# The first raw loads of the mixer's weights wait for a left operand of group 4

## The chip, the cores and the metric

The kernel runs on one NeuronCore of a Trainium2 chip. Its engines work side by side: TensorE (PE in the profile; its weight loads are PEld) multiplies matrices, VectorE (DVE), ScalarE (ACT) and GpSimd (POOL) work elementwise, and SyncE (SP) issues most DMA transfers. DMA issues also stand in ScalarE's queue (ACTq). An engine runs its instructions in order, and a DMA whose data or buffer isn't ready holds up what is queued behind it on the same issuing queue. The metric is the device time of one execution in microseconds. Before the change its median is 1780.38 us over 3 runs (1780.27 to 1782.05).

## The reference

One decoder layer on x of 1024 tokens by 1024 features, in float32:

```python
x = layernorm(ALPHA * x + 0.5 * swiglu(x, ffn1_w1, ffn1_w3, ffn1_w2))
m = mixer(x, w_in, ..., w_uk, w_uv, ..., ws, bs, w_out)
x = layernorm(ALPHA * x + m)
x = layernorm(ALPHA * x + 0.5 * swiglu(x, ffn2_w1, ffn2_w3, ffn2_w2))

def swiglu(x, w1, w3, w2):          # hidden width 2816
    return (silu(x @ w1) * (x @ w3)) @ w2
```

The mixer projects x with `w_in`, runs sparse attention (an indexer picks 256 of the causal keys per query, the attention works on latent keys and values of width 128) on one half and a chunked gated MLP on the other, and projects the result with `w_out`.

## The kernel before

**Splits.** A float32 product is made of three matmuls on split operands: `split` writes hi = the operand rounded to the matmul's format (ScalarE, L87) and lo = operand - hi (VectorE or GpSimd, L88), and `mm3` (L149 to L153) adds hi x hi, hi x lo and lo x hi in one PSUM tile.

**Stage 1 of the first feed-forward part** computes silu(x w1) * (x w3) in 11 groups (NG) of hidden columns. In each group a 2x2 block product is done with 7 block products instead of 8; the left operands are sums of the w13 weights (four loads of 512 KB per group, L341, issued one group ahead; sums in `left`, L287 to L292; then their split), the right operands are sums of x, made once (`xs`). A block product is 24 matmuls. For groups 0 to 5 the products m = 1 and 2 are computed ahead of all else ("early"; the results are spilled and read back, L433 and L434), so these groups have 5 products left, in the order 6, 7, 5, 4, 3 (group 0: 6, 5, 7, 3, 4); groups 6 to 10 have 7, in the order 1, 6, 2, 7, 5, 4, 3. There are two pairs of PSUM banks (`ab`), so a product waits until VectorE has added up the product two before it: L381 takes product 6, L412 and L415 use products 7 and 5, L422 product 4, L428 product 3 (group 0 has L392 to L405 for some of these). `gated` (L348, L349) applies silu and the product, `out` (L439 to L449) forms the seven sums of the hidden block and stores them to DRAM (`f`).

**The mixer's weights** are split ahead of time, beside stage 1. `make_parts` is a generator over 29 weights. For each it issues the load of the next raw weight on SP (L116, up to 512 KB), splits the present one on ScalarE and VectorE (tile `made`) and stores the pair to DRAM from ScalarE's queue (L136, up to 1 MB). `product` calls it four times per block product (L329, L330), one step each; six steps make one weight. A list scheduler then sets the order on each engine by dependences and estimated times, so that a load which depends on nothing can move ahead of where it was written.

**Buffers.** Raw weights and the `hid` loads of stage 2 share one ring of two buffers (`raw`, N_W = 2), in program order. The split pairs, the `xs` pairs and the W2 weights share a pool of 15 large buffers.

**Stage 2** multiplies by W2: 11 loads of 1 MB (L503, `w_446` to `w_456`), loads of the stored hidden sums (`hid`, L551, two pieces of 256 KB in one), their splits into a and b, and W2 sums on VectorE (L524, L525). Its pieces (m, k) are worked in a fixed order, (1,0), (1,1), (1,2) and so on, with 12 matmuls each (tile y for these).

Of the kernel before, what the change touches and what calls it, by code (L numbers as in the profile page):

```python
# [7 lines left out]
F32 = mybir.dt.float32  # L8
# [5 lines left out]
ALU = mybir.AluOpType  # L14
# [17 lines left out]
N_W = PAR["NW"]  # L32
N_BIG = PAR["NB"]
EARLY = 6
class Net:
# [63 lines left out]
    def make_parts(self):  # L99

        nc, ins = self.nc, self.ins
        flat = lambda x: x.rearrange("p k c -> p (k c)")
        todo = [(("T", i), flat(ins["w_inT"][i])) for i in (6, 4, 5)]
        todo += [((n, j), flat(ins["w_in" + n][j])) for n in "ABC" for j in range(4)]
        todo += [("ws", flat(ins["wsT"]))]
        todo += [(("T", i), flat(ins["w_inT"][i])) for i in range(2)]
        todo += [(("O", i), ins["w_out"][i]) for i in range(4, 8)]
        todo += [(("T", i), flat(ins["w_inT"][i])) for i in range(2, 4)]
        todo += [("wuk", flat(ins["w_ukT"]))]
        todo += [(("O", i), ins["w_out"][i]) for i in range(4)]  # L110
        raws = {}

        def load(i):
            if i < len(todo):
                raws[i] = self.raw("made", (P, todo[i][1].shape[-1]))
                nc.sync.dma_start(raws[i], todo[i][1])  # L116

        load(0)
        for i, (key, src) in enumerate(todo):
            x, n = raws[i], src.shape[-1]  # L120
            load(i + 1)
            if key == "ws":
                y = x.rearrange("p (g c) -> p g c", g=NH)
                nc.gpsimd.affine_select(
                    out=y, in_=y, pattern=[[0, NH], [1, P]], compare_op=ALU.is_ge, fill=0.0, base=0, channel_multiplier=-1
                )
            if key == "wuk":
                nc.scalar.activation(x, x, AF.Copy, scale=0.125)
            yield
            t = self.large("made", (P, 2, n))  # L130
            self.split(x, t[:, 0], t[:, 1])
            yield
            yield
            name = self.name("made")
            self.made[key] = self.dram.tile([P, 2, n], F32, tag=name, name=name)
            nc.scalar.dma_start(self.made[key], t.bitcast(F32))  # L136
            for _ in range(3):
                yield
# [117 lines left out]
    def ffn(self, name, w13, w2, begin, meanwhile, load_acc, norm, after, side=iter(())):  # L256
# [21 lines left out]
        def left(n):  # L278

            for g, m in plan[len(lefts) : n]:  # L280
                if g < EARLY and m in (1, 2):
                    lefts[g, m] = self.parts(first_blocks[g, m], V)
                    continue
                a = blocks[g]
                if m == 6:
                    a[5] = self.page("S", (P, 2, HALF))
                    V.tensor_tensor(a[5], a[7], a[4], ALU.add)  # L287
                    a[6] = a[1]
                    V.tensor_tensor(a[7], a[1], a[7], ALU.subtract)
                    V.tensor_tensor(a[6], a[5], a[1], ALU.subtract)  # L290
                if m == (5 if g else 3):
                    V.tensor_tensor(a[2], a[2], a[6], ALU.subtract)  # L292
                    a[3] = a[2]
                lefts[g, m] = self.parts(a[m], E(PAR["LE"][m - 1] if g > 1 else 0))

        def halves(j):

# [16 lines left out]
        def product(g, m, ps, start=True):  # L314
            now = plan.index((g, m))
            for k in range(4):
# [9 lines left out]
                for j in range(2):  # L326
                    ks = slice(k * P, (k + 1) * P)
                    self.mm3(ps[:, j], (w[0][:, j, ks], w[1][:, j, ks]), x, start and k == 0, k == 3, m in (1, 2, 3, 5))
                if g > 1 and now > 2 * EARLY:  # L329
                    next(side, None)  # L330

        def load(g, m, s=slice(0, 2), of=None):
# [901 lines left out]
```

## Time and profile before

| | |
|---|---|
| median of 3 runs | 1780.38 us |
| the profiled execution's own time | 1782.18 us |
| its span on the core | 1780.5 us |
| TensorE busy | 1728.8 us (97%) |
| VectorE busy | 1330.2 us (75%) |
| ScalarE busy | 792.0 us (44%) |
| GpSimd busy | 394.1 us (22%) |
| mean DMA rate | 163 GB/s |

The profile shows one execution. Its span runs from the first to the last instruction on the core, and the time of that execution is 1.7 us longer. Busy times of the engines overlap. A wait names the instruction that released it. Line numbers are those of the kernel before; in the changed kernel the lines from L116 on are 3 higher and those after the left operands 4 higher (the raw load is L119, the L88 split is unmoved, L381 is L385, L503 is L507, L551 is L555).

### The profile page before, as it was taken

The numbers are of one execution on the slowest core, as the hardware profiler recorded it, in microseconds if no ns is written. First come the engines' busy times: TensorE is split into PE (matmuls) and PEld (weight loads), VectorE is DVE, ScalarE is ACT, GpSimd is POOL, SyncE is SP. The second block draws the span as 40 slices with busy tenths as digits, with TensorE's granted clock in tenths as the row PEclk, the third lists the DMA queues.
The fourth block names the chain that finished last, engine by engine and source line by source line (L and its number), as shares of the span: only waits on it lengthen the run. The fifth ranks groups of instructions, "written<-read, shape, count | busy, mean of one in ns | idle before, by whom it ended". The sixth has DMA issues, their size and how long they took to land.

```text
span 1780.5 us, 22284 instructions
## 1 busy us (share of the span) xinstructions
PE 1728.8 (97%) x8056; PEld 1449.9 (81%) x8056; DVE 1330.2 (75%) x2213; ACT 792.0 (44%) x1328; POOL 394.1 (22%) x287
## 2 busy tenths in 40 slices
PE   8989999999999999999978999999999999999997
PEld 6878888888888889998866888888788888888886
DVE  5778886765895864699889877877877555589586
ACT  5433333333654524568687662452313222354551
POOL 0004332222000460011246421100423222200036
PEclk9999999999999999999999999999999999999999
DMA  7458777758545342225412006435443322753532
GB/s 285 154 213 318 256 262 276 280 204 305 192 122 173 107 184 95 96 84 198 169 36 95 1 1 212 154 119 188 157 178 121 136 89 89 288 195 118 181 101 83
DMA packets 90141, 289.96 MB, mean 163 GB/s; under 512 B 9136, under 2 KB 9648, under 8 KB 85680
## 3 DMA queue, kind: packets, MB, share of 16 engines
q1 hardware_dynamic: 82496, 253.12, 40.1%
q10 hardware_dynamic: 5616, 32.54, 4.6%
q0 software_dynamic: 1920, 2.89, 0.8%
q8 instruction: 63, 1.03, 0.2%
q14 instruction: 46, 0.38, 0.1%
HBM read 195.94 MB, written 89.69 MB: 160 GB/s over the span
## 4 chain that ended last, share of the span: by engine, by line
PE 71%; DVE 7%; ACT 4%; DMA 2%; issue 2%; POOL 1%; SPq 0%; POOLq 0%; ACTq 0%; DVEq 0%
PE ab L151 11%; PE ab L153 11%; PE ab L152 11%; PE y L152 5%; PE y L153 5%; PE y L151 5%; PE z L153 3%; PE z L152 3%; PE z L151 3%; ACT act L828 2%; PE pN L153 2%; PE pN L151 2%; PE pN L152 2%; PE tr L1006 1%; PE lg L702 1%
## 5 line engine op out<-in xcount | busy, mean ns | idle before, releaser
L151 PE MATMUL ab<-xs,hi 128*128 128x512 f32 x1232 | 482.4, 392 | 18.4 <-DVE c L415 6.7
L152 PE MATMUL ab<-xs,hi 128*128 128x512 f32 x1232 | 481.2, 391 | 0.0
L153 PE MATMUL ab<-xs,lo 128*128 128x512 f32 x1232 | 481.0, 391 | 0.0
L151 PEld LDWEIGHTS ab<-xs,hi 128*128 128x128 f32 x1232 | 232.6, 189 | 69.7 <-issue 12.5
L152 PEld LDWEIGHTS ab<-xs,hi 128*128 128x128 f32 x1232 | 232.6, 189 | 48.9 <-DVE xs L88 0.4
L153 PEld LDWEIGHTS ab<-xs,lo 128*128 128x128 f32 x1232 | 232.5, 189 | 48.6
L88 POOL TENSOR_TENSOR lo<-w,hi 128x1024 fp32r<-128x1024 f32 x54 | 137.9, 2553 | 568.6 <-ACT hi L87 531.2
L87 ACT ACTIVATE hi<-w 128x1024 fp32r<-128x1024 f32 (+1 forms) x134 | 137.6, 1040 | 160.4 <-DVE w L290 126.6
L88 DVE TENSOR_TENSOR lo<-w,hi 128x1024 fp32r<-128x1024 f32 (+1 forms) x80 | 94.7, 1195 | 42.4 <-ACT hi L87 41.9
L88 DVE TENSOR_TENSOR a<-hid,a 128x512 fp32r<-128x512 f32 x132 | 93.3, 707 | 24.2 <-ACT a L87 24.0
L87 ACT ACTIVATE a<-hid 128x512 fp32r<-128x512 f32 x132 | 82.0, 621 | 53.9 <-DMA hid<-f 50.2
L153 PE MATMUL z<-b,a 128*128 128x512 f32 x264 | 102.7, 389 | 0.0
L152 PE MATMUL y<-b,a 128*128 128x512 f32 x264 | 102.7, 389 | 0.0
L153 PE MATMUL y<-b,a 128*128 128x512 f32 x264 | 102.7, 389 | 0.0
L152 PE MATMUL z<-b,a 128*128 128x512 f32 x264 | 102.7, 389 | 0.0
L151 PE MATMUL z<-b,a 128*128 128x512 f32 x264 | 102.5, 389 | 0.0
L88 DVE TENSOR_TENSOR b<-w,b 128x512 fp32r<-128x512 f32 x110 | 77.1, 701 | 34.0 <-ACT b L87 33.8
L828 ACT ACTIVATE act<-score,tk 128x768 int8<-128x768 f32 (+2 forms) x93 | 87.0, 935 | 34.2 <-DVE tk L840 27.7
L151 PE MATMUL y<-b,a 128*128 128x512 f32 x264 | 102.0, 389 | 0.0
L87 ACT ACTIVATE b<-w 128x512 fp32r<-128x512 f32 x110 | 68.4, 622 | 51.9 <-PE z L153 38.5
L348 ACT ACTIVATE h<-c 128x512 f32<-128x512 f32 x34 | 21.4, 631 | 152.8 <-DVE c L415 103.3
L592 POOL TENSOR_TENSOR xacc<-xacc,T 128x512 f32<-128x512 f32 x8 | 13.0, 1652 | 333.8 <-DVE T L565 333.8
(264 smaller groups left out, 3586.7 us busy)
## 6 DMA issues: line engine op xcount, KB each, us to landing
w<-in_ffn_w_dram SPq DMA_DIRECT2D x110, 512.0 KB, 6.3
hid<-f SPq DMA_DIRECT2D x60, 512.0 KB, 3.8
w<-in_ffn_w_dram SPq DMA_DIRECT2D x22, 1024.0 KB, 10.3
made<-made ACTq DMA_DIRECT2D x17, 1024.0 KB, 6.3
f<-h SPq DMA_DIRECT2D x32, 512.0 KB, 3.6
f<-c SPq DMA_DIRECT2D x22, 512.0 KB, 3.1
wo<-made SPq DMA_DIRECT2D x8, 1024.0 KB, 6.9
xr<-x_spill SPq DMA_DIRECT2D x16, 512.0 KB, 5.6
```

What stands on the lines that cost most here:

```text
L87: nc.scalar.activation(hi, src, AF.Copy)
L88: (eng or nc.vector).tensor_tensor(lo, src, hi.bitcast(F32), ALU.subtract)
L151: mm(out, a[0], b[0], start=start, stop=False, skip_group_check=skip)
L152: mm(out, a[0], b[1], start=False, stop=False, skip_group_check=skip)
L153: mm(out, a[1], b[0], start=False, stop=stop, skip_group_check=skip)
L348: nc.scalar.activation(t, c[:, 0], AF.Silu)
L592: nc.gpsimd.tensor_tensor(acc[j][:, HALF:], acc[j][:, HALF:], T[j], ALU.add)
L702: self.nc.tensor.matmul(out, l, r, start=n == 0, stop=n == 1)
L828: nc.scalar.activation(out, s, AF.Sign, bias=fj, scale=-1.0, accum_out=val[:, j : j + 1])
L1006: nc.tensor.transpose(pt[:, hh * P : (hh + 1) * P], ps4[hh][:, j * P : (j + 1) * P], self.ident)
```

## The change

`left` remembers the hi tile of the last left operand that it made (`self.recent`). For the first two raw loads, GpSimd first writes two columns of the raw buffer (hi - hi of that operand), so that the DMA, which overwrites them, has to wait for it. And `product` begins to call the generator in group 4 instead of group 2. When the first call comes, the last operand made is that of group 4, product 4.

```diff
@@ make_parts
             if i < len(todo):
                 raws[i] = self.raw("made", (P, todo[i][1].shape[-1]))
+                if i < N_W:
+                    t = self.recent.bitcast(F32)[:, 0, :2]
+                    nc.gpsimd.tensor_tensor(raws[i][:, :2], t, t, ALU.subtract)
                 nc.sync.dma_start(raws[i], todo[i][1])
@@ left
                 lefts[g, m] = self.parts(a[m], E(PAR["LE"][m - 1] if g > 1 else 0))
+                self.recent = lefts[g, m][0]
@@ product
-                if g > 1 and now > 2 * EARLY:
+                if g > 3 and now > 2 * EARLY:
                     next(side, None)
```

The order of SP's queue around the four w13 loads of group 2 before (`w_110` to `w_113`; `made` are raw loads of the mixer's weights):

```order
L444 DMA f_75<-u_88_651 128x512
L341 DMA w_110_834<-in_ffn_w_dram 128x1024
L341 DMA w_111_836<-in_ffn_w_dram 128x1024
L341 DMA w_112_838<-in_ffn_w_dram 128x1024
L448 DMA f_75<-c_89_652 128x1024
L448 DMA f_75<-h_90_653 128x1024
L341 DMA w_113_840<-in_ffn_w_dram 128x1024
L116 DMA made_1121<-in_w_inA_dram 128x768
L116 DMA made_1172<-in_w_inA_dram 128x768
L449 DMA f_75<-u_88_651 128x512
```

The same place in the changed kernel:

```order
L345 DMA w_110_834<-in_ffn_w_dram 128x1024
L345 DMA w_111_836<-in_ffn_w_dram 128x1024
L345 DMA w_112_838<-in_ffn_w_dram 128x1024
L452 DMA f_75<-c_89_652 128x1024
L452 DMA f_75<-h_90_653 128x1024
L345 DMA w_113_840<-in_ffn_w_dram 128x1024
L453 DMA f_75<-u_88_651 128x512
L448 DMA f_75<-h_104_784 128x512
```

The raw loads behind and between the groups' loads are gone here; the loads of w13 stand behind the same store (`f<-c`).

SP's queue before, at the first hid loads and the first W2 load (`w_446`), in groups 8 and 9:

```order
L116 DMA made_2613<-in_w_out_dram 128x1024
L551 DMA hid_3126<-f_75 128x2x512
L446 DMA f_75<-h_359_2396 128x1024
L551 DMA hid_3140<-f_75 128x2x512
L448 DMA f_75<-c_374_2477 128x1024
L448 DMA f_75<-h_375_2478 128x1024
L449 DMA f_75<-u_373_2476 128x512
L503 DMA w_446_3100<-in_ffn_w_dram 128x2x1024
L341 DMA w_409_2735<-in_ffn_w_dram 128x1024
```

In the changed kernel, where the last two raw loads and the W2 loads stand in the last group:

```order
L119 DMA made_2958<-in_w_out_dram 128x1024
L555 DMA hid_3128<-f_75 128x2x512
L507 DMA w_446_3102<-in_ffn_w_dram 128x2x1024
L507 DMA w_447_3104<-in_ffn_w_dram 128x2x1024
L507 DMA w_448_3106<-in_ffn_w_dram 128x2x1024
L507 DMA w_449_3108<-in_ffn_w_dram 128x2x1024
L507 DMA w_450_3110<-in_ffn_w_dram 128x2x1024
L507 DMA w_451_3112<-in_ffn_w_dram 128x2x1024
L507 DMA w_452_3114<-in_ffn_w_dram 128x2x1024
L507 DMA w_453_3116<-in_ffn_w_dram 128x2x1024
L507 DMA w_454_3118<-in_ffn_w_dram 128x2x1024
L555 DMA hid_3142<-f_75 128x2x512
```

The first hid load now comes behind the last raw load, the W2 loads come behind the first hid load, and the second hid load (`hid_3142`) behind the ninth W2 load (`w_454`).

VectorE's order in the last group before (L381, L412, L415 add products 6, 7 and 5; a and b are splits for stage 2):

```order
L381 TENSOR_TENSOR c_431_2912<-ab_2915,c_431_2912 128x1024
L349 TENSOR_TENSOR h_432_2914<-h_432_2914,ab_2883 128x512
L412 TENSOR_TENSOR u_438_2976<-ab_2979,c_431_2912 128x1024
L415 TENSOR_TENSOR c_439_2977<-ab_3009,u_438_2976 128x1024
L349 TENSOR_TENSOR h_440_2978<-h_440_2978,c_439_2977 128x512
L88 TENSOR_TENSOR a_3128<-hid_3126,a_3128 128x512
L88 TENSOR_TENSOR b_3131<-w_446_3100,b_3131 128x512
L88 TENSOR_TENSOR a_3134<-hid_3126,a_3134 128x512
```

And in the changed kernel, where the last four splits of the mixer's weights (numbers 26 to 29) stand among the same additions:

```order
L88 TENSOR_TENSOR made_2850<-made_2791,made_2850 128x1024
L385 TENSOR_TENSOR c_423_2895<-ab_2898,c_423_2895 128x1024
L88 TENSOR_TENSOR made_2918<-made_2842,made_2918 128x1024
L353 TENSOR_TENSOR h_424_2897<-h_424_2897,ab_2864 128x512
L88 TENSOR_TENSOR made_2966<-made_2910,made_2966 128x1024
L416 TENSOR_TENSOR u_435_2971<-ab_2974,c_423_2895 128x1024
L88 TENSOR_TENSOR made_3019<-made_2958,made_3019 128x1024
L419 TENSOR_TENSOR c_436_2972<-ab_3006,u_435_2971 128x1024
L353 TENSOR_TENSOR h_437_2973<-h_437_2973,c_436_2972 128x512
L88 TENSOR_TENSOR a_3130<-hid_3128,a_3130 128x512
```

The split of weight 28 (`made_2966`, from the raw tile `made_2910`) now stands between the additions of products 6 and 7 of the last group.

## Rows read from the trace of the kernel before

**Rows 1.** Head of the page: span; busy us (share) and instructions per engine.

```profile
span 1780.5 us, 22284 instructions
...
PE 1728.8 (97%) x8056; PEld 1449.9 (81%) x8056; DVE 1330.2 (75%) x2213; ACT 792.0 (44%) x1328; POOL 394.1 (22%) x287
```

**Rows 2.** TensorE's waits: line and releaser: us in total, times, longest.

```profile
PE qa L702 <- DVE ql L694: 8.1, 2, 5.4
PE ab L151 <- DVE c L415: 6.7, 2, 5.2
...
PE ab L151 <- DVE u L381: 1.7, 2, 0.9
...
PE ab L151 <- DVE c L428: 1.1, 1, 1.1
```

**Rows 3.** Timeline of TensorE: start us, us, instruction [idle before <-releaser].

```profile
104.35 0.47 PE L151 MATMUL ab<-xs,hi 128*128 128x512 f32 x1 [0.57 <-DVE c L405]
...
125.99 0.39 PE L153 MATMUL ab<-xs,lo 128*128 128x512 f32 x1
131.60 0.76 PE L151 MATMUL ab<-xs,hi 128*128 128x512 f32 x1 [5.22 <-DVE c L415]
```

**Rows 4.** Windows: length, busy us (matmuls, ...) per engine, granted clock, DMA share, GB/s.

```profile
420.00:440.00 20.00, 20.00 (x90) 16.57 (x89) 8.96 (x13) 6.34 (x11) 2.39 (x1) 1.00 1.02 412
...
126.40:130.70 4.30, 0.00 (x0) 0.00 (x0) 4.23 (x5) 1.79 (x2) 0.00 (x0) 1.00 0.00 0
130.70:137.50 6.80, 5.90 (x14) 4.67 (x15) 6.80 (x5) 3.99 (x5) 4.29 (x2) 0.50 0.58 205
...
102.00:124.00 22.00, 21.43 (x95) 17.42 (x94) 14.90 (x16) 6.02 (x7) 0.00 (x0) 1.00 0.95 338
```

**Rows 5.** Timeline of VectorE, left operands of group 2 and the addition L415.

```profile
124.19 1.23 DVE L287 TENSOR_TENSOR S<-w,w 128x1024 f32<-128x1024 f32 x1 [7.29 <-DMA w<-in_ffn_w_dram]
...
130.24 1.22 DVE L415 TENSOR_TENSOR c<-ab,u 128x1024 f32<-128x1024 f32 x1
```

**Rows 6.** Timeline of SP's queue, 78 to 124 us.

```profile
82.02 20.28 SPq L116 DMA_DIRECT2D made<-in_w_inT_dram  x3
...
111.48 1.15 SPq L341 DMA_DIRECT2D w<-in_ffn_w_dram  x1
```

**Rows 7.** Timeline of TensorE, end of stage 1 and start of stage 2.

```profile
442.20 0.39 PE L151 MATMUL ab<-xs,hi 128*128 128x512 f32 x1
...
442.88 0.39 PE L151 MATMUL y<-b,a 128*128 128x512 f32 x1
```

**Rows 8.** Timeline of SP's queue, last groups of stage 1.

```profile
378.23 0.38 SPq L503 DMA_DIRECT2D w<-in_ffn_w_dram  x1
...
413.30 19.26 SPq L503 DMA_DIRECT2D w<-in_ffn_w_dram  x8
436.70 5.11 SPq L551 DMA_DIRECT2D hid<-f  x2
```

**Rows 9.** DMA issues of the whole run: KB each, median us to landing.

```profile
made<-made ACTq DMA_DIRECT2D x17, 1024.0 KB, 6.3
...
made<-in_w_out_dram SPq DMA_DIRECT2D x8, 512.0 KB, 5.9
```

**Rows 10.** Timeline of ScalarE and VectorE, the split of one mixer weight.

```profile
271.92 1.06 ACT L87 ACTIVATE made<-made 128x1024 fp32r<-128x1024 f32 x1 [2.79 <-DMA made<-made]
...
273.02 1.23 DVE L88 TENSOR_TENSOR made<-made,made 128x1024 fp32r<-128x1024 f32 x1 [4.11 <-ACT made L87]
```

**Rows 11.** DMA issues on the page (its part 6).

```profile
f<-h SPq DMA_DIRECT2D x32, 512.0 KB, 3.6
```

**Rows 12.** Costliest groups on the page: busy us, mean ns of one | idle before.

```profile
L88 DVE TENSOR_TENSOR a<-hid,a 128x512 fp32r<-128x512 f32 x132 | 93.3, 707 | 24.2 <-ACT a L87 24.0
L87 ACT ACTIVATE a<-hid 128x512 fp32r<-128x512 f32 x132 | 82.0, 621 | 53.9 <-DMA hid<-f 50.2
```

**Rows 13.** DMA issues from 411 to 434 us.

```profile
f<-h SPq DMA_DIRECT2D x1, 512.0 KB, 10.2
```

## Prediction

> **What bounds the kernel now.** I read the head of the page first. TensorE is busy for 1728.8 us of a span of 1780.5 us [rows 1], so a change can win only gaps of TensorE and its half-speed stretches, and what it can lose is a new gap. The list of TensorE's waits shows the gaps: in the matmuls of the first feed-forward part (tile ab) 6.7 us for the addition of product 5 (L415), two of 0.8 and 0.9 for L381, one of 1.1 for L428, and in the attention 8.1 us for ql [rows 2]. The timeline of TensorE places the longest: after the matmul at 125.99 the next one starts at 131.60, and it takes 0.76 instead of 0.39 us [rows 3]. The windows show the rest: in 126.4 to 130.7 TensorE did nothing, and in 130.7 to 137.5 the granted clock is 0.50, so 1.2 GHz, and 14 matmuls fill 5.90 us [rows 4].
>
> Then I follow this wait back. On VectorE the addition L415 starts at 130.24; five operations on the left operands of group 2 stand ahead of it, the first at 124.19 after 7.29 us of waiting for a load of w13 weights [rows 5]. On SP's queue that load is the last of four for group 2, issued at 111.48; three raw loads of the mixer's weights held the queue from 82.02 to 102.30 [rows 6]. In 102 to 124 the DMA engines are busy for 0.95 of the time, at 338 GB/s [rows 4].
>
> At the other end of the stage there is no wait today: matmuls follow each other from the last products of stage 1 into stage 2, whose first y matmul starts at 442.88, and the pitch is (442.88 - 442.20) / 3 = 0.2267 us [rows 7]. A product of 24 matmuls takes 5.44 us, a group of seven 38.1 us, so the last group starts at T = 442.88 - 38.1 = 404.8.
>
> **The change, part by part.** It adds two subtractions of 128x2 on GpSimd, and they make the first two raw loads wait for the left operand of group 4, product 4. GpSimd is busy for 394.1 of 1780.5 us [rows 1], so the two cost nothing themselves even if each took a microsecond. What I price are the waits: the raw loads, the splits on ScalarE and VectorE and the stores of 29 weights move from groups 0 to 8 into groups 4 to 10.
>
> Gain, first stall. The raw loads leave SP's queue in groups 0 and 1, and their traffic goes from 102 to 124. The spacing 125.99 to 131.60 falls from 5.61 to 0.23, which is 5.38. The 14 matmuls at half clock give back 5.90 - 14 x 0.2267 = 2.73. The 0.57 us at 104.35 [rows 3], 0.7 with its long first matmul, goes with a made split ahead of L405 on VectorE. That is 8.8. What is late next is the same w13 load: it is issued behind a store (f<-c, L448) that waits for the group's results and does not move. Without a made store of 1 MB and two raw loads of 0.5 MB beside it, 5.1 us at the 412 GB/s of [rows 4], I estimate that it lands at 119 instead of 124.2. From landing to the end of L415 were 7.3 us (124.19 to 131.46 [rows 5]), so L415 ends at 126.3, where TensorE is ready at about 125.7: 0.6 of the stall remains.
>
> Gain, small stalls. The first L381 stall (0.8) stands in group 4, behind a made split of group 3, which has none afterwards: 0.8. The second L381 stall (group 5) and the L428 stall (group 8) have a made split ahead of them afterwards as before: 0. Groups 6, 7 and 9 carry 5, 5 and 6 splits instead of 4, 4 and none. The bounds are the whole 2.8 as a gain, and as much as a loss. Gain together 8.8 - 0.6 + 0.8 = 9.0 (5.4 to 11.6).
>
> Loss, start of stage 2. The two raw buffers serve the mixer's weights and the hid loads of stage 2 in turn, and they come free later now. Before, the first hid loads stand ahead of the first W2 load, which goes out at 378.23; the last eight of the eleven W2 loads (1 MiB each) are issued from 413.30, and the third hid load at 436.70 [rows 8]. After, two raw loads stand ahead of the first hid load, this one ahead of nine W2 loads, and the second hid load behind these. A raw load takes its buffer when the weight two before it is split. One such step is a load of 5.9 us [rows 9], a split of 1.06 on ScalarE and 1.23 on VectorE [rows 10] and some 0.1 of signals: 8.3 us. The split of weight 24 stands just behind the start of the last group, so the load of weight 26 goes out at about T+3. Two steps later, at T + 3 + 16.6 = T+19.6, weight 28 is split, its buffer is free, and the hid load and the W2 loads go out. Before, eight of them were let go from 413.30 = T+8.5, and the others earlier.
>
> The W2 loads fill the DMA engines: in 420 to 440 their share is 1.02, at 412 GB/s [rows 4]. At that rate 1 MiB (1.049 MB) takes 2.55 us. Ahead of the second hid load are 0.5 + 9 MiB, it is 0.5 MiB itself: 10 x 2.55 = 25.5. Two stores of made weights on ScalarE's queue (1 MiB each, 6.3 us in the median [rows 9]) share the engines in that time: 5.1. For issue and completion I take 2, an estimate from the 3.6 us of a 0.5 MiB store [rows 11], of which 1.3 are transfer at 412 GB/s. It lands at 19.6 + 25.5 + 5.1 + 2 = T+52.2. Piece (1,2) needs it split: ScalarE 0.62 and VectorE 0.71 [rows 12], and about one VectorE operation ahead of it, 0.6: 1.9 in sum. TensorE is there at T + 38.1 + 2 x 2.72 = T+43.5 (a piece has 12 matmuls). It waits 54.1 - 43.5 = 10.6. The lower end leaves the stores, the operation ahead and 0.6 of the start out: 46.5 + 1.3 - 43.5 = 4.3. The upper end has one more half step, 14. No work hides it, since the pieces are worked in a fixed order, and what is queued behind this load on SP waits too. The third hid load is behind w_455, w_456 and a store of 0.5 MiB; with itself 3 MiB, 7.7 us, against 5.44 of two pieces, so another 2.2 (0 to 2.2).
>
> Loss, clock. The wait of 5.22 us was followed by 14 matmuls at a granted clock of 0.50, a loss of 2.7; the wait of 0.57 only by one matmul of 0.47 [rows 3]. A wait of 10 us is nearer to the first: 2.7 (0 to 3.4). Loss together 10.6 + 2.2 + 2.7 = 15.5 (4.3 to 19.6).
>
> The order in the attention moves too. Its largest wait is the 8.1 us for ql [rows 2]; I see no reason for a sign and take 0, with 2 either way.
>
> The sum against the profiled execution, which took 1782.2 us with a span of 1780.5: + 15.5 - 9.0 = + 6.5, 1788.7. That execution is 1.8 above the median of 1780.4, so the forecast is 1786.9.
>
> The trace moves 412 GB/s while W2 loads run [rows 4]. The Trainium skill ("DMA: Bandwidth & Descriptors", Specifications) gives about 358 GB/s as what one core gets from its memory. By that figure 1 MiB would take 2.93 us, the 12 MiB up to the second hid load 4.6 us more, and the result would be about 1791. The measurement decides.
>
> **Rivals.** (a) The forecast, slower by 6.5: the last raw loads hold the first hid load, this holds W2, and W2 holds the second hid load.
>
> (b) The same jam at its lower end: 4.3 + 2.2 + 2.7 = 9.2 against 9.0, so 1780.6. For it: the last splits could come earlier, since VectorE has idle time, and the made stores could be spread wider. Against it: a DMA share of 1.02 leaves nothing free. It decides if the second hid load lands before T+47.
>
> (c) The second hid load does not wait its turn behind the nine W2 loads. Then only the 2.2 of the third remain, and the time is 1780.4 - 9.0 + 2.2 = 1773.6, faster. For it: it is 0.5 MiB against 1 MiB, spread over the same engines. Against it: a store of 0.5 MiB (f<-h) issued among the W2 loads takes 10.2 us to land [rows 13], against 3.6 in the median [rows 11]; it waited its turn. I give this 0.18. The Trainium skill ("DMA: Bandwidth & Descriptors", Queues, rings and completion order) calls completion "not FIFO per issuing engine", which is the rule that this rival would follow; the 10.2 us speak against it here.
>
> (d) The change does not remove the stall at 126, because the w13 load is late by itself, behind its store and three others. Then the gain is 0.7 + 0.8, and the time is 1780.4 + 15.5 - 1.5 = 1794.4. For it: the load goes out only at 111.48, and four of 0.5 MiB need 5.1 us. Against it: it took 12.7 us to land, with only four such loads in flight.
>
> **Numbers.** 0.2% (3.6 us) is about what a measurement of this kernel can tell from no change. (a) 0.48, of which 0.05 ends within 0.2%; (b) 0.26, of which 0.05 faster, 0.16 the same and 0.05 slower; (c) 0.18; (d) 0.08. Faster is 0.05 + 0.18 = 0.23, same 0.05 + 0.16 = 0.21, slower 0.43 + 0.05 + 0.08 = 0.56. The likeliest case alone spans 1782 to 1792. The range over all goes from (c), 1773, to 1792 and leaves out (d) and the tails.
>
> **What would show it.** After the change: no wait of several microseconds near 126 to 131 and no stretch at 0.50 there; no raw load of the mixer's weights on SP before group 4; the first hid load and nine W2 loads from about T+20; a wait of 4 to 14 us in the y matmuls, ended by a split (L88) that waits for a hid load; a low clock behind it. The forecast is wrong if W2 loads go out by T+10, if the second hid load lands long before the ninth W2 load, or if a wait stays at 131.

## The result and the profile after

The changed kernel took 1802.57 us (median of 4 runs, 1797.9 to 1804.71), the kernel before in the same comparison 1780.41 (1780.27 to 1782.05): a ratio of 1.0113, 95% interval 1.0100 to 1.0126. It is slower, as forecast, but by 22 us instead of 6.5, and the time lies above the range of 1773 to 1792. The profiled execution took 1800.83 us, with this head of the page:

```profile
span 1799.1 us, 22309 instructions
...
PE 1734.9 (96%) x8056; PEld 1454.2 (81%) x8056; DVE 1328.4 (74%) x2213; ACT 793.9 (44%) x1328; POOL 394.5 (22%) x289
```

The engines' work is that of [rows 1]; of the 18.6 us by which the span grew, 6.1 us are longer busy time of TensorE, from matmuls at the lower clock, and the rest is idle time. TensorE's list of waits (total, times, longest) has a new head:

```profile
PE y L154 <- ACT b L87: 17.3, 1, 17.3
PE ab L154 <- ACT xs L87: 6.7, 1, 6.7
PE ab L154 <- DVE c L419: 4.6, 2, 2.6
...
PE y L154 <- ACT T L590: 3.2, 1, 3.2
PE qa L706 <- DVE ql L698: 2.8, 1, 2.8
PE ab L154 <- DVE c L432: 2.2, 2, 1.2
PE ab L154 <- DVE u L416: 2.0, 1, 2.0
PE ab L154 <- DVE h L353: 1.7, 2, 1.2
```

(L419 is the L415 of [rows 2].) The wait of 5.2 has become one of 2.6, ql has lost 5.3, and one wait of 17.3 us has come. TensorE works its matmuls in the same order in both kernels up to the attention, so the start of the same matmul can be subtracted, after less before; where the order differs, the n-th matmul of each is taken. Where the difference steps:

| place (us in the changed kernel) | after - before, us |
|---|---|
| first matmul | +1.2 |
| 103.34, start of group 1 | -1.0 |
| 131.14, end of group 1, behind the old stall | -6.5 |
| 225.89, group 5 | -8.7 |
| 340.38, group 8 | -4.8 |
| end of stage 1 | -0.9 |
| behind the wait of 17.3 and its slow matmuls | +19.6 |
| behind the wait for T (L590), product 2 of stage 2 | +25.8 |
| end of the attention | +16.3 |
| end | +18.6 |

So five pieces: a gain of 8.7, near the 9.0 predicted; 7.9 of it given back in groups 6 to 10; 20.4 + 6.3 = 26.7 lost at the start of stage 2; 9.5 won from there to the end of the attention; 2.3 lost behind it. Before rounding the sum is -8.73 + 7.88 + 26.68 - 9.52 + 2.28 = 18.59.

**The first stall.** TensorE at the place of [rows 3], and the windows of [rows 4] in the changed kernel (length, busy of PE, PEld, DVE, ACT, POOL, granted clock, DMA share, GB/s):

```profile
127.87 0.47 PE L154 MATMUL ab<-xs,hi 128*128 128x512 f32 x1 [2.60 <-DVE c L419]
```

```profile
126.40:130.70 4.30, 2.83 (x13) 2.37 (x14) 3.95 (x5) 2.94 (x4) 1.28 (x1) 1.00 0.00 0
130.70:137.50 6.80, 6.80 (x32) 5.63 (x31) 4.95 (x3) 1.69 (x3) 6.38 (x3) 1.00 0.62 186
```

The wait is halved and the stretch at the half clock behind it has gone. On VectorE the first left operand of group 2 now starts at 120.43 instead of 124.19 [rows 5]; its load went out at 110.61 and landed at 120.41. The change moves it: before group 4 no raw load is on SP, the first goes out at 190.10.

**The start of stage 2.** SP's queue in the last group of stage 1; T, the start of that group, is 400.0 here:

```profile
406.32 1.46 SPq L119 DMA_DIRECT2D made<-in_w_out_dram  x2
...
414.35 4.62 SPq L119 DMA_DIRECT2D made<-in_w_out_dram  x2
428.24 0.38 SPq L555 DMA_DIRECT2D hid<-f  x1
428.71 17.97 SPq L507 DMA_DIRECT2D w<-in_ffn_w_dram  x9
447.06 2.01 SPq L555 DMA_DIRECT2D hid<-f  x1
```

The first hid load waits for weight 28's buffer until T+28.2, nine W2 loads follow it, the second hid load comes behind them. It landed at 463.74, the ninth W2 load at 462.38. What that does to TensorE (timeline), and the windows around it:

```profile
464.96 2.08 PE L154 MATMUL y<-b,a 128*128 128x512 f32 x4 [17.33 <-ACT b L87]
```

```profile
430.00:447.00 17.00, 17.00 (x69) 13.93 (x68) 12.40 (x17) 4.09 (x7) 0.00 (x0) 0.90 1.02 386
447.00:464.90 17.90, 0.63 (x3) 0.19 (x1) 2.14 (x4) 1.14 (x3) 0.00 (x0) 0.60 1.03 408
464.90:471.00 6.10, 6.04 (x14) 4.82 (x15) 4.52 (x8) 1.05 (x3) 0.00 (x0) 0.51 1.03 414
```

From 430 to 471 the DMA engines are never idle, as in 420 to 440 before [rows 4]; but now TensorE stands still for 17.3 of it, and 14 matmuls at a clock of 0.51 follow. The second, smaller wait has its cause on ScalarE, shown here from 494 on:

```profile
494.02 0.63 ACT L87 ACTIVATE a<-hid 128x512 fp32r<-128x512 f32 x1 [2.68 <-DMA hid<-f]
494.55 0.61 ACT L87 ACTIVATE b<-w 128x512 fp32r<-128x512 f32 x1
495.07 2.04 ACT L590 ACTIVATE T<-y 128x512 f32<-128x512 f32 x4
```

The copies of finished sums out of PSUM (L590) stand in ScalarE's order behind a split that waits for a later hid load; TensorE waits for the bank and starts at 495.70.

### The profile page after: what moved, and what is told of

Read it like the earlier page. It is cut to its first block, busy times and chain, and to the rows that moved or that the text cites. A ratio compares the mean times of both kernels' runs of the same rounds, so it can differ in the third digit from the quotient of the medians.

```text
span 1799.1 us, 22309 instructions
## 1 busy us (share of the span) xinstructions
PE 1734.9 (96%) x8056; PEld 1454.2 (81%) x8056; DVE 1328.4 (74%) x2213; ACT 793.9 (44%) x1328; POOL 394.5 (22%) x289
## 4 chain that ended last, share of the span: by engine, by line
PE 68%; DVE 11%; DMA 11%; ACT 5%; issue 3%; POOL 1%; SPq 1%; POOLq 0%; ACTq 0%; DVEq 0%
PE ab L154 11%; PE ab L156 11%; PE ab L155 11%; DMA made<-made 5%; PE y L154 4%; PE y L155 4%; PE y L156 4%; DMA w<-in_ffn_w_dram 3%; PE z L155 3%; PE z L156 3%; PE z L154 3%; ACT act L832 2%; PE pN L156 2%; PE pN L154 2%; PE pN L155 2%
## 5 line engine op out<-in xcount | busy, mean ns | idle before, releaser
L154 PE MATMUL ab<-xs,hi 128*128 128x512 f32 x1232 | 482.5, 392 | 19.6 <-ACT xs L87 6.7
L154 PE MATMUL y<-b,a 128*128 128x512 f32 x264 | 99.5, 400 | 20.5 <-ACT b L87 17.3
```

The source lines that it names most:

```text
L154: mm(out, a[0], b[0], start=start, stop=False, skip_group_check=skip)
```

## The experiments

Letters in the expectations name theories as they stood at the time. Ratios are to the kernel before on the same chip. "After" is the changed kernel.

### Starting earlier, or without the dependence

start_g1 keeps the wait and lets the generator begin in group 2; start_g2 begins in group 3; no_dependence begins in group 4 without the two GpSimd operations.

```diff
-                if g > 3 and now > 2 * EARLY:
+                if g > 1 and now > 2 * EARLY:      # start_g1;  g > 2 in start_g2
```
```diff
-                if i < N_W:                          # no_dependence, from after
-                    t = self.recent.bitcast(F32)[:, 0, :2]
-                    nc.gpsimd.tensor_tensor(raws[i][:, :2], t, t, ALU.subtract)
```

> The changed kernel, with the generator called from group 2 on (g > 1, as before); the wait of the first two raw loads for the last left operand made is kept, it is now one of group 2. Theory A (the wait itself is good, 29 weights in seven groups are too dense): the first stall near 131 us goes (about 8 us), the last raw load is issued some 25 us before the last group, the W2 loads go out by T+8 (T: start of the last group), no wait at y (1,2); 1770 to 1776 us. Rival B (what costs is the wait on GpSimd, or the order that a real dependence brings, wherever it stands): still a wait of over 5 us at the start of stage 2 or in groups 6 to 9, over 1785 us.

> The changed kernel with the generator called from group 3 on (g > 2), wait kept. Theory A: the first stall goes as well; the last raw load is issued about T-2, the split of weight 29 is done about T+8, the second hid load stands behind four W2 loads instead of nine and lands by T+30, before it is needed at T+43; of the give-back in groups 6 and 7 (3.9 us in the changed kernel) about as much stays; 1773 to 1780 us. Rival B: over 1790 us, since each group of delay costs alike.

> Only the later call of the generator (g > 3), without the GpSimd writes: the raw loads depend on nothing. Theory A: the scheduler puts the loads and splits back into groups 0 and 1, the stall near 131 us stays (4 to 6 us), no wait at stage 2; 1777 to 1784 us, the same as before. Rival C (the position in the program alone moves the loads): a loss of 10 us or more at stage 2, over 1790 us.

start_g1: 0.9971 (0.9961 to 0.9981), 1777.69 against 1783.18 us, a little faster than before, but short of theory A's 1770 to 1776. start_g2: 1.0098 (1.0083 to 1.0113), 1799.8 us. Theory A misses it. Rival B's number is met, its reason isn't: from start_g1 to start_g2 one group of delay cost 22 us, from there to the changed kernel about 3. no_dependence: 1.0003 (0.9992 to 1.0014), as theory A had it.

Without the dependence nothing moves: the scheduler takes the raw loads forward to where they were, and TensorE still waits 5.07 us at 131.06. So the dependence does the moving, and the group alone would not. With it, start_g1 has no wait in the first product of stage 2, since its chain is done in time; 1.78 us for T remain in product 2. SP's queue there (T = 406.5):

```profile
409.37 0.38 SPq L507 DMA_DIRECT2D w<-in_ffn_w_dram  x1
413.25 0.37 SPq L555 DMA_DIRECT2D hid<-f  x1
413.72 0.42 SPq L507 DMA_DIRECT2D w<-in_ffn_w_dram  x1
...
417.64 17.05 SPq L507 DMA_DIRECT2D w<-in_ffn_w_dram  x9
438.82 0.37 SPq L555 DMA_DIRECT2D hid<-f  x1
```

W2 goes out from T+2.9, and the second hid load ahead of all but one of them. start_g2 moves the second hid load behind four W2 loads only, but its third hid load stands behind the last W2 loads, and a wait of 11.07 us appears two pieces later, at (1,4).

### Which resource holds the second hid load: queue, ring or bandwidth

w2_gpsimd_queue issues W2 from GpSimd's queue; own_ring gives the hid loads two buffers of their own (and takes two pages for them, NP 21 to 19); own_ring_raw_on_act issues the raw loads from ScalarE's queue besides.

```diff
-            nc.sync.dma_start(W[k], w2[2 * k : 2 * k + 2]...)
+            nc.gpsimd.dma_start(W[k], w2[2 * k : 2 * k + 2]...)
```
```diff
-        return self.work.tile(list(shape), F32, tag="w", bufs=N_W, ...)
+        return self.work.tile(list(shape), F32, tag="wh" if s in ("hid", "wuv") else "w", bufs=N_W, ...)
```
```diff
-                nc.sync.dma_start(raws[i], todo[i][1])
+                nc.scalar.dma_start(raws[i], todo[i][1])
```

> The changed kernel with the eleven W2 loads issued from GpSimd's queue, so that no hid load stands ahead of them or behind them on SP. Theory A: the W2 loads go out as their buffers come free, the hid loads wait only for the raw buffers (T+24 and T+32 in the trace of the changed kernel); the wait of 17.3 us at y (1,2) falls to 0 to 5 us, the second low-clock stretch and the 3.2 us wait go with it; 1775 to 1785 us. Rival D (it is bandwidth, not the queue: 11 MiB and the stores need the time wherever they are issued): the wait stays at 10 us or more, over 1792 us.

> The changed kernel, but the hid loads of stage 2 (and one small weight of the attention) have two raw buffers of their own, paid with two of the 21 pages (19). The first two hid loads then wait for no mixer's weight and go out before group 9; the W2 loads stand on SP only behind the last raw load (T+14 in the trace of the changed kernel, where T is 404) instead of T+24. Theory A (the last raw loads hold hid and W2, and a late burst of W2 costs its delay beyond some slack): the wait of 17.3 us at y (1,2) is gone, at most 5 us at y (1,4), where the third hid load is behind w_456; 1776 to 1786 us. Rival D (the burst's traffic is what costs, with all DMA engines full from T+8 on): a wait of 10 us or more remains, over 1790 us.

> The kernel own_ring with the raw loads of the mixer's weights issued from ScalarE's queue, so that nothing of these weights stands on SP ahead of W2. Theory A: the W2 loads go out when their buffers come free, from T-30 to T+8 as before the change; no wait over 1.5 us at the start of stage 2; 1772 to 1780 us. Rival D: as own_ring, since the same bytes move in the last group.

1.0120 (1.0105 to 1.0135), 1.0073 (1.0055 to 1.0091), 1.0092 (1.0075 to 1.0108): none is back at the kernel before, theory A misses all three, and Rival D's times are met. With W2 on another queue the one long wait breaks into several (two for b of 9.1 in sum, one for T of 4.7), and the DMA engines are full for 58 us (windows with the columns of above):

```profile
412.00:430.00 18.00, 17.01 (x76) 13.78 (x75) 6.63 (x6) 6.04 (x7) 11.67 (x10) 1.00 1.02 395
430.00:446.00 16.00, 10.82 (x48) 8.62 (x46) 5.15 (x6) 2.90 (x5) 1.86 (x3) 0.95 1.01 395
446.00:470.00 24.00, 19.50 (x73) 15.25 (x73) 18.77 (x31) 7.53 (x15) 1.43 (x2) 0.86 1.03 410
```

So the order of SP's queue decides where the wait stands, and taking W2 off it does not remove the wait. Whether the bytes or their late start make it, this run doesn't tell: on GpSimd's queue W2 stood behind a subtraction (422.88 to 425.28) and left at 425.22, T+23.9, only 4.8 us sooner than in after. own_ring shows the same of the order: its hid loads don't wait for a raw buffer, the wait at piece (1,2) is gone, and one of 14.65 stands at (1,4), for the third hid load, which follows the W2 loads on SP:

```profile
417.17 25.88 SPq L507 DMA_DIRECT2D w<-in_ffn_w_dram  x11
444.04 1.67 SPq L555 DMA_DIRECT2D hid<-f  x1
```

```profile
461.91 0.79 PE L154 MATMUL y<-b,a 128*128 128x512 f32 x1 [14.65 <-ACT b L87]
```

With the raw loads on ScalarE's queue, W2 waits on SP behind stores of results and leaves at 420.64; TensorE waits 7.21 and 2.13.

### The lo halves on GpSimd

Both kernels take the splits' subtraction from VectorE to GpSimd; made_split_gpsimd starts from after, g1_split_gpsimd from start_g1.

```diff
-            self.split(x, t[:, 0], t[:, 1])
+            self.split(x, t[:, 0], t[:, 1], nc.gpsimd)
```

> The changed kernel with the low halves of the mixer's weights made on GpSimd instead of VectorE. The changed kernel lost 3.9 us in groups 6 and 7 and 3.7 us in the last group; theory A: it does because such a split waits for its raw load in VectorE's order, ahead of an addition that TensorE needs; with GpSimd these 7.6 us go, as long as GpSimd's own left operands (2.5 us each, about 4 per group) do not become late; the jam at stage 2 stays or is 2 to 5 us worse, as a split takes 2.5 instead of 1.2 us; 1794 to 1801 us. Rival E (the losses in groups 6 to 10 come from the traffic or from VectorE's plain load): they stay, 1801 to 1808 us.

> start_g1 with the low halves of the mixer's weights made on GpSimd. Start_g1 lost about 6 us between groups 3 and 10 in small stalls of TensorE behind such splits. Theory A: they go, without a jam at stage 2: 1770 to 1775 us, the fastest so far. Rival E: no gain against start_g1 (1777.7), or a loss where GpSimd is late with left operands: 1777 to 1790 us.

1.0249 (1.0228 to 1.0269) and 1.0083 (1.0065 to 1.0101): both much slower, against every theory. For 128x1024 GpSimd's form takes 2.43 us on average where VectorE's takes 1.23 [rows 10], the chain ends later still, and the waits for b in stage 2 grow to 35.5 us in three (in g1_split_gpsimd 7.93 for one b and 4.16 for T). It shows the price of a later chain; that VectorE's time was the limit it does not show.

### Less to do in the last group

no_last_four leaves the last four weights (w_out 0 to 3) out and reads the copies of the other four in their place. late_four_g3 and late_four_g1 make these four in stage 2 instead, held back by a GpSimd write on a stage-2 operand, with a page as raw buffer and lo on GpSimd; late_four_big loads them straight into a large buffer.

```diff
-        todo += [(("O", i), ins["w_out"][i]) for i in range(4)]
...
+        for j in range(4):
+            self.made["O", j] = self.made["O", j + 4]      # no_last_four
```
```diff
+        todo = todo[25:] if late else todo[:25]             # late_four_g3, _g1 (with g > 1)
...
+        more = self.make_parts(True) if name == "f1" else iter(())
...
+                if m in (2, 6, 5):
+                    next(more, None)
```
```diff
+            t = self.large("made", (P, 2, 1024))            # late_four_big, with g > 1
+            nc.sync.dma_start(t[:, 1].bitcast(F32), self.ins["w_out"][i])
...
+            self.split(t[:, 1].bitcast(F32), t[:, 0], t[:, 1], nc.gpsimd)
```

> The changed kernel without the last four of the 29 mixer's weights (the half of the output projection that belongs to the attention): they are not loaded, split or stored, and the mixer reads the other half's copies in their place. In the last group four raw loads (2 MiB) and four to five stores (4 to 5 MiB) are gone, and nothing of the mixer's stands on SP ahead of hid and W2. Theory F (bytes: from the start T of the last group until the W2 burst has landed the DMA engines are full, and the third hid load is behind the burst): 6 to 7 MiB less is 15 to 18 us less, the burst ends by T+42, and no wait over 1 us is left at the start of stage 2; 1772 to 1777 us, as the gain in groups 1 to 5 (8.7) stays, less some 4 given back in groups 6 to 9. Rival G (the loss at stage 2 has another source, such as the place of the hid loads in ScalarE's order): 3 us or more of waits remain there, over 1782 us.

> The changed kernel with the last four of the mixer's weights made in stage 2, from its second product on, each raw load held back by a GpSimd write that depends on an operand of stage 2, the raw weights in page buffers, low halves on GpSimd. All work is done. Theory F: as no_last_four up to the second product, then four loads and stores beside DMA engines that are half idle there: 1772 to 1779 us. Rival H (moved, not gone: the four weights now hold hid loads or pages in stage 2): a wait of over 3 us at products 2 to 5 of stage 2, over 1782 us.

> As late_four_g3, with the generator of the first 25 weights called from group 2 on. Theory F: the first stall is gone as in start_g1 (1777.7 beside a before of 1783.2), the chain of raw loads ends four weights earlier, so that no traffic of it is left near stage 2: 1 to 4 us faster than start_g1, a ratio of 0.994 to 0.997 to before. Rival H: the same ratio as start_g1 or worse, 0.997 to 1.003, with new waits in stage 2.

> late_four_g1 with the four raw loads going straight into the large buffer of their pair (no page, no raw buffer), all four issued early in the second product of stage 2, their splits three pieces apart and on GpSimd. The 6 us of waits that late_four_g1 had near 528 us, behind a raw load and a split that waited for a page, go: ratio to before 0.993 to 0.997, 1771 to 1778 us beside a before of 1783. If it is the traffic itself that hurts there, waits of over 3 us remain between 470 and 560 us and the ratio is 0.998 or more.

1.0032 (1.0021 to 1.0043), 1.0051 (1.0032 to 1.0070), 1.0001 (0.9992 to 1.0010), 0.9991 (0.9982 to 1.0000). Without the four weights the loss at the start of stage 2 is 8.5 us instead of 26.7: these four cost 18.2 there, more than half of the loss. Their bytes and their hold on the hid loads go together here, so the run doesn't part the two. W2 goes out from T+8.1; waits of 3.69 us at (1,4) and 2.54 for T remain, so theory F's time of 1772 to 1777 is missed (1789.33) and Rival G's waits are there.

Made in stage 2 they cost what they save, as Rival H says. late_four_g3 still waits 3.40 us at (1,4) and 1.68 for T, and 3.0 in four waits in the third product. late_four_g1 has no wait in the first two products, and 4.5 + 1.5 us in the third, where a late split on ScalarE waits 7.11 us for its raw load, and this load for a GpSimd write that took 8.36.

late_four_big has waits of 1.16 and 3.93 at 503 to 508, and its ratio is the one expected if the traffic itself hurts there. None comes to start_g1's time.

### Which buffer sets the pace of the chain

My prediction took the two raw buffers. raw3 gives them a third (and takes a page, NP 21 to 20); big16 gives the large buffers a sixteenth (and takes two pages, NP 21 to 19). Each ran on after (g3), on start_g1 (g1) and on the kernel before.

```diff
-PAR = {'NP': 21, 'NW': 2, 'NB': 15, ...
+PAR = {'NP': 20, 'NW': 3, 'NB': 15, ...      # raw3
+PAR = {'NP': 19, 'NW': 2, 'NB': 16, ...      # big16
```

> The changed kernel with three raw buffers instead of two, paid with one of the 21 pages. All bytes stay; in SP's order three hid loads now stand ahead of most of the W2 loads (before w_446 and before w_450). Theory J (place: TensorE waits for a hid load queued behind the W2 burst): the waits of 17.3 us at y (1,2) and at (1,4) go, the remaining one, if any, is at (1,6) and under 6 us; the chain of raw loads has one more buffer, so the 3.9 us of groups 6 and 7 shrink to under 2; 1778 to 1788 us. Theory K (bytes: the DMA engines are full from T to T+55 whatever the order): a wait of over 10 us in all at the start of stage 2, over 1790 us.

> start_g1 with three raw buffers and 20 pages. Theory J: some of the 6 us that start_g1 gives back in groups 3 to 7 stay won; ratio to before 0.993 to 0.997. Theory K: as start_g1, 0.997 to 1.000, or worse by what the page is worth.

> The kernel before with three raw buffers and 20 pages: the control. Theory J and K: the first stall stays (the raw loads still go out in group 0), 1778 to 1786 us, a ratio of 0.998 to 1.002; if the page matters, it shows here as a loss.

1.0087 (1.0071 to 1.0102), 1.0017 (1.0008 to 1.0026), 0.9999 (0.9990 to 1.0008). A third raw buffer doesn't free the chain. In raw3_g3 the wait moves once more, to 8.20 us at (1,6) for the fourth hid load; groups 6 and 7 give back 3.7 us still, where after gave back 3.9, and the last group loses 7.1 (a wait of 3.76 for L416 and slow matmuls behind it). raw3_before shows that a page less costs the kernel before nothing; raw3_g1 is slower than start_g1 by more than either interval, where theory J had it faster. raw3_g3's time is in theory K's range, not in J's. Why the third buffer doesn't help stands in ScalarE's splits around 255 in after (timeline; in raw3_g3 the same three rows come a microsecond earlier, with waits of 2.04 and 7.74):

```profile
253.69 0.85 ACT L87 ACTIVATE made<-made 128x768 fp32r<-128x768 f32 x1 [1.92 <-DMA made<-made]
256.97 0.36 ACTq L139 DMA_DIRECT2D made<-made  x1
262.30 0.85 ACT L87 ACTIVATE made<-made 128x776 fp32r<-128x776 f32 x1 [7.77 <-DMA made<-made]
```

The releaser is not a raw load, which would read made<-in_w_...: it is the store of the pair before, DRAM made from SBUF made. The store issued at 256.97 landed at 262.22, the split starts at 262.30; the one before landed at 253.66, its split started at 253.69; the same at 303.31 and 303.33. The raw load for the split at 262.30 had landed at 253.15, nine microseconds before. And so it goes through groups 4 to 9: from the second weight to the 23rd every split starts 0.02 to 0.11 us after the store of the pair before has landed. By the program 14 of the 15 large buffers hold `xs` pairs there, so one is free for pairs, and the next pair waits until the last one is in DRAM: one weight in 8.6 us (253.69 to 262.30). Meanwhile VectorE, in order, holds its additions behind the lo of that weight (its timeline in after):

```profile
256.86 1.21 DVE L385 TENSOR_TENSOR c<-ab,c 128x1024 f32<-128x1024 f32 x1
263.18 0.97 DVE L88 TENSOR_TENSOR made<-made,made 128x776 fp32r<-128x776 f32 x1 [5.11 <-ACT made L87]
264.07 0.68 DVE L353 TENSOR_TENSOR h<-h,ab 128x512 f32<-128x512 f32 x1
```

> The changed kernel with 16 large buffers instead of 15 and 19 pages instead of 21, two raw buffers. Theory L (one large buffer for pairs, held until its store has landed, sets the pace): two weights overlap, a step falls from 8 us towards the split and the raw load, the splits no longer wait for a store in VectorE's order; the give-back in groups 6 to 9 (3.9 us in the changed kernel) falls under 1.5 us, the last raw load goes out before the last group, W2 from about T+3, no wait over 2 us at the start of stage 2; 1770 to 1778 us. Rival M (density itself: the same splits and bytes in seven groups cost VectorE and the DMA engines the same): a loss of 10 us or more against before remains, over 1790 us.

> start_g1 with 16 large buffers and 19 pages. Theory L: the small stalls of start_g1 in groups 3 to 9 (about 6 us) halve, ratio to before 0.992 to 0.996. Rival M: as start_g1 (0.997) or worse by what two pages are worth.

> The kernel before with 16 large buffers and 19 pages, the control. Its raw loads still go out in group 0, so the first stall stays: 0.998 to 1.002 of before. Theory L: its small stalls in groups 4, 5 and 8 (2.9 us) shrink; Rival M: no change or a loss.

0.9989 (0.9977 to 1.0001), 1.0081 (1.0066 to 1.0096), 1.0149 (1.0126 to 1.0173). big16_g3, the changed kernel with one more large buffer, ends at 1779.57 us instead of 1802.57. ScalarE's splits there at the same time, weights 12 to 14, where after has come to its 7th:

```profile
254.84 0.85 ACT L87 ACTIVATE made<-made 128x768 fp32r<-128x768 f32 x1 [1.11 <-DMA made<-made]
...
260.64 0.85 ACT L87 ACTIVATE made<-made 128x768 fp32r<-128x768 f32 x1
...
264.45 0.85 ACT L87 ACTIVATE made<-made 128x768 fp32r<-128x768 f32 x1 [2.97 <-DVE made L88]
```

From 254.84 to 264.45 that is one weight in 4.8 us. From the 2nd weight to the 29th (191.78 to 364.74) a step takes 6.4 us, in after (206.08 to 428.68) 8.2. SP's queue:

```profile
358.51 0.33 SPq L119 DMA_DIRECT2D made<-in_w_out_dram  x1
...
362.51 6.11 SPq L555 DMA_DIRECT2D hid<-f  x2
...
371.75 3.16 SPq L507 DMA_DIRECT2D w<-in_ffn_w_dram  x2
...
399.22 3.10 SPq L507 DMA_DIRECT2D w<-in_ffn_w_dram  x2
...
411.96 9.39 SPq L507 DMA_DIRECT2D w<-in_ffn_w_dram  x6
428.16 5.11 SPq L555 DMA_DIRECT2D hid<-f  x2
```

The last raw load goes out 60 us earlier than in after (358.51, against 418.63), two hid loads and four W2 loads are out before the burst, and the third hid load lands at 434.8. The difference of the table above is -8.5 for this kernel from the start of group 6 through the start of stage 2 (-7.1 for a while around the start of group 8): no give-back, no wait for a hid load. Some 7 us are lost again by the last matmul, 4.0 of them from 1147 to 1163 in the second feed-forward part and 1.5 at 1742; 19 pages instead of 21 are a possible cause, but that was not isolated. The expectation's 1770 to 1778 us is missed by 1.6, its signs in stage 1 and at stage 2 are there. Two things limit what this shows. The scheduler's order moves with the buffer, so pace on the chip and place in the program were not changed apart. And the buffer helps only here; big16_g1 and big16_before miss theory L (0.992 to 0.996 and 0.998 to 1.002) by far, and Rival M had named a loss without its size: with an early start (big16_g1) TensorE has stalls of 1.97, 2.11, 2.58 and 3.41 in groups 3 to 7, for which no cause was shown, and in the kernel before it makes TensorE's waits for L415 17.7 us in five, against 6.7 in two [rows 2].

**The runs together.** At what time after T the last W2 load and the hid load behind the W2 loads land, and what TensorE waits for it:

| kernel | W2 burst issued, T+ | last W2 landed, T+ | that hid load landed, T+ | wait, us |
|---|---|---|---|---|
| before | 6.6 to 27.4 (9) | 38.3 | 39.6, third | 0 |
| start_g1 | 11.2 to 27.9 (9) | 43.7 | 45.0, third | 0 |
| no_last_four | 8.1 to 31.3 | 50.2 | 51.5, third | 3.7 at (1,4) |
| own_ring | 20.0 to 44.1 | 62.2 | 63.5, third | 14.65 at (1,4) |
| raw3_g3 | 25.2 to 48.3 | 66.8 | 69.4, fourth | 8.2 at (1,6) |
| after | 28.7 to 52.1 | 68.7 | 63.7, second | 17.3 at (1,2) |

(9) stands for the last nine of the eleven loads, where the first two went out apart from them. The later the last W2 load is issued, the later it lands; the queue's order picks the piece that meets it.

## Why the prediction was right and where it was wrong

**Right in size, in part by luck: the gain.** 9.0 was worked out, 8.7 measured. Its parts are off and cancel. The stall with its clock gave 5.5 where 7.5 were reckoned; the L381 stall of group 5, priced at 0, gave 1.1, and group 4's 1.1 instead of 0.8. 2.6 us of the stall remain, not 0.6, mostly since the load landed at 120.4 and not at 119, and L419 ended as much later than reckoned; the clock behind it came back as said. Rival (d) is out as a whole, though a little of it was true: the load is still late without that traffic (DMA share 0.45 in 100 to 124, where it was 0.87 before).

**Right: the place and kind of the loss.** First hid load behind the raw loads, nine W2 loads behind it, the second hid load behind these, TensorE waiting at (1,2), a stretch at a granted clock of 0.51 behind it. Rival (c) is out: the second hid load landed 1.36 us after the ninth W2 load, issued ahead of it. The clock term, 2.7, was 2.9 at that wait. The bound for (b), T+47, was passed by 16.7.

**Wrong: the size, in the step "Loss, start of stage 2".** I said: "A raw load takes its buffer when the weight two before it is split ... 8.3 us", and "T+19.6". Measured T+28.2. The raw load of weight 26 left at T+6.3, not T+3 (+3.3): the split of weight 24 began at T+2.5, but VectorE's half of it ended only at T+6.2. The first step took 8.0 (-0.3), the second 13.9 (+5.6). That second raw load took 11.5 us from issue to landing and not the 5.9 of [rows 9], the median of loads which mostly run on engines with room. While it ran (414.35 to 425.87) two more raw loads, three stores of pairs and three stores of results were under way; the last four raw loads took 5.7, 8.8, 11.5 and 9.5 us in turn. In the window the DMA share is 0.91, and ScalarE waited for the third of them:

```profile
414.00:428.00 14.00, 13.40 (x60) 10.76 (x58) 4.38 (x5) 3.67 (x5) 4.83 (x2) 1.00 0.91 364
```

```profile
425.89 1.06 ACT L87 ACTIVATE made<-made 128x1024 fp32r<-128x1024 f32 x1 [5.31 <-DMA made<-in_w_out_dram]
```

I counted the traffic for the W2 loads and not for the raw loads ahead of them. From the release to the landing of the second hid load were 35.5 us where I had 32.6; the loads and stores of the stretch (issued in 404 to 465) show what ran beside each other, with the median time to landing:

```profile
w<-in_ffn_w_dram SPq DMA_DIRECT2D x11, 1024.0 KB, 18.0
made<-made ACTq DMA_DIRECT2D x6, 1024.0 KB, 8.8
made<-in_w_out_dram SPq DMA_DIRECT2D x4, 512.0 KB, 9.1
...
hid<-f SPq DMA_DIRECT2D x3, 512.0 KB, 14.8
```

That makes 8.6 + 2.9 = 11.5 us later than T+52.2. From landing to matmul were 1.2 us instead of 1.9, and TensorE itself came to (1,2) at T+47.6 instead of T+43.5, mostly through the stalls of the last group: 10.6 + 11.5 - 0.7 - 4.1 = 17.3.

**The whole miss.** + 6.5 was forecast, + 18.6 measured. The wait at (1,2) with its clock took 20.4, not 13.3; the give-back of 7.9 and the wait for T with its clock, 6.3, were not priced, and neither were 2.3 behind the attention; the third hid load's 2.2 did not come. Against that stand 9.5 won up to the end of the attention, for which I had 0. So the sum of the losses was further off than the time shows.

**Wrong beneath it: what paces the chain.** In groups 4 to 9 the raw buffers are not what holds its steps; the one free large buffer and its store are. The releasers show it, with the sixteenth buffer the loss is gone (its order moved too), and with the third raw buffer it isn't. In the last group, from weight 26 on, where large buffers come free, the raw load is the releaser, as my step has it. That my 8.3 us a step comes near the 8.2 of the whole chain is luck: most of those steps are made of a store. [rows 10] had it: the split of the kernel before waits 2.79 us for "DMA made<-made", a store, and my step has none in it.

**Wrong: "Gain, small stalls".** Groups 6 and 7 gave back 3.9 us, the last group, which that sum left out, 3.9 (a wait of 2.00 at 429.40 for L416 and slow matmuls behind it). The bound of 2.8 was too narrow: with splits in order on VectorE, a wait for a store (5.11 us at 263.18) lies ahead of TensorE's additions.

**Not foreseen.** The wait for T in product 2, with its clock 6.3 us. I followed the hid loads to the first piece that needs them, not to what stands on ScalarE behind the splits of the later ones. The third hid load's 2.2, which I did price, did not come: it landed at 471.29, and TensorE began (1,4) at 473.33 without a wait. And 9.5 were won up to the end of the attention, where I had 2 at most; ql's waits fell by 5.3 of that, to 2.8. start_g1 won 8.4 on the same stretch (ql's waits 2.7), start_g2 1.2 (7.4), with the same work: an effect of the order which these runs do not explain. Without it the loss would have been about 28.

**A version that beats both.** start_g1 (the dependence, beginning in group 2): 0.9971 of the kernel before. In the profiled executions (1780.65 against 1782.18) it is 5.0 us ahead of the kernel before behind the first stall, gives all of that back in small stalls (L385, L432, L353), stands 2.1 behind at the end of stage 1, and is ahead at the end only by the 8.4 won up to the end of the attention. So its gain is not the removed stall's, and it is of the kind that another order could take away.

## What to carry to other kernels

A chain that prepares data beside other work can go no faster than its scarcest buffer, the time of its store included: read from the waits of its first instruction which buffer that is, and look at whether the releaser's source is DRAM or SBUF. Delaying such a chain is free only if its end stays clear of the next burst of loads; work out that end from durations measured in a full stretch, not from the median over the run. A start that is moved in the program text moves nothing if a scheduler may take it back; a real dependence does. And a gain that is measured can stand elsewhere than where it was sought: subtract the start of the same matmul through the whole trace, as for start_g1.

## What the runs showed of the hardware

- **Clock.** The wait of 2.60 us at 127.87 (2.79 at 129.37 in start_g1) was followed by windows at a granted clock of 1.00, that of 2.00 at 429.40 by 0.67 in the next 1.6 us and 0.87 from 431 to 440. The length of the wait alone doesn't tell which comes.
- **DMA.** 386 to 414 GB/s for 41 us without a pause, reads from memory for the most part, so again more than the limit of about 358 GB/s that the Trainium skill gives for one core ("DMA: Bandwidth & Descriptors", Specifications).
- **VectorE beside GpSimd.** In after an operation of 128x512 on VectorE took 2.90 us instead of 0.69, when GpSimd had begun one just before (250.90 to 253.32):

```profile
250.37 0.69 DVE L445 TENSOR_TENSOR h<-h,h 128x512 f32<-128x512 f32 x1
250.97 2.90 DVE L446 TENSOR_TENSOR u<-c,h 128x512 f32<-128x512 f32 x1
```

It ends 0.55 us after GpSimd's, so most of its work came behind that. The Trainium skill ("SBUF — State Buffer", Who interferes with whom) says that a VectorE instruction with two SBUF inputs contends with a GpSimd instruction that reads SBUF, and that the order of issue decides which of them blocks; the trace agrees.
